# Low weight parts of the q, k and v projections by an accumulating transfer from GpSimd, high products first

## The chip, the cores and the metric

The kernel runs on one core of one Trainium2 chip. The metric is the device time of one execution in microseconds; several executions are timed and their median is given. A profile of one more execution shows what each engine did: PE (TensorE, matmuls), PEld (its weight loads), DVE (VectorE), ACT (ScalarE), POOL (GpSimd) and SP (SyncE, which here only issues DMAs).

## The reference

One encoder block with two token mixers side by side (a gated delta rule in both directions and a Fourier mixer), merged by gates, and an MLP with squared ReLU. T = 256 tokens, width 2048, all in float32. What bears on this case is the projection of the normed input and the delta rule branch:

```python
h = rms_norm(x, g_mix[l])
proj = h @ w_in[l]
q, k, v, z, f, scal, gates = jnp.split(proj, SPLIT_POINTS, axis=-1)
y_a = gated_deltanet_branch(q, k, v, z, scal, conv_w[l], ...)
...
# in the branch: convolution over 5 tokens, silu, heads of 128, then per chunk
m = jnp.where(strict, jnp.einsum("bhnid,bhnjd->bhnij", kb, k) * decay, 0.0)
a_mat = m + jnp.eye(CHUNK, dtype=m.dtype)
rhs = jnp.concatenate([v * beta, kb * jnp.exp(gc)[..., None]], axis=-1)
sol = lax.linalg.triangular_solve(a_mat, rhs, left_side=True, lower=True, unit_diagonal=True)
```

q, k and v have 1024 columns each, in 8 heads of 128.

## The kernel before

**Split products.** Each float32 matrix is split into a high part in fp32r (a rounded copy) and a low part (the rest), and a product is made of three: high by high, high by low and low by high. The input's parts are `h_hi` and `h_lo`. The weights come in pieces of 512 KB (128 x 1024 elements): SP loads a piece into a tile `raw`, `split` (L87) makes `hi` on ScalarE by a copy (L88) and `lo` on VectorE as raw - hi (L92), and PE multiplies. `wtiles` (L96) gives the tiles: four buffers for `raw`, three for `hi`, three for `lo`, shared by all the projections in turn.

**The q, k and v projections** are made by `pair_fm` (L104) for two head tiles at a time. A head tile has 2048 x 128 weights, two pieces (q = 0 and 1), and each piece 24 products of 128 x 256 that accumulate into one half of a PSUM bank: for each of 8 blocks L121 (high by high), L122 (high by low) and L127 (low by high). Five chunks of four heads come this way (40 pieces, 960 matmuls); the first chunk of k goes through `stream_k0` and isn't touched. `qkv_chunk` (L307) takes the sums from PSUM (L321), with GpSimd's memsets of the borders of `u` ahead of that, and convolves on ScalarE and VectorE (L324, L326). `stream` (L156) makes the other projections: z, the gates, and more.

**The delta rule** works on two groups of four heads (`dn_group`, L618). For each, `dn_k`, `dn_v` and `dn_q` project and norm, `dn_decay` makes the decays E, and `dn_inv` (L443) inverts the blocks: products of k (L463), the compact matrix Kc goes out to DRAM and comes back as Mf (L474, L481), 31 steps of two VectorE instructions (L489, L491) solve the 32 x 32 blocks, the solution Xf goes out and back as Xh (L493, L498), becomes Xc (L500), De and DT (L505 to L508), and PE joins the blocks (L521, L528, L540, L544), with copies between (L524, L532). `dn_out` (L560) makes the outputs (L574 to L601). z is projected between the groups (`z_chunk`).

**What sets the order.** The framework's scheduler orders each engine's instructions by a plan of its own before the program is built, across all of these functions. On the chip each engine works through its list in order, and waits at the first instruction whose inputs or buffers aren't ready. So a change in one function moves instructions of others too.

Of the kernel before, what the change touches and what calls it, by code (L numbers as in the profile page):

```python
# [8 lines left out]
F32 = mybir.dt.float32  # L9
F32R = mybir.dt.float32r  # L10
AF = mybir.ActivationFunctionType
ALU = mybir.AluOpType
PSUM = bass.MemoryType.PSUM

P = 128
# [12 lines left out]
def encoder_block_kernel(ctx, tc, xT, x, g_mix, w_qkv, w_k0, w_in, w_g, w_sc, conv_w, hprm, g_head, w_dn, w_fo, w_o,  # L28
                         g_mlp, w_up, w_down, g_fin, tri, dft, out, dbg=None):
    nc = tc.nc  # L30
    dve, act, pool, pe = nc.vector, nc.scalar, nc.gpsimd, nc.tensor
# [13 lines left out]
    def mm_ps():  # L45
        return psm.tile([P, NW], F32, tag="mm", name=nm("mm"))
# [40 lines left out]
    def split(hi, lo, src, scale=1.0, src2=None):  # L87
        act.activation(hi, src, AF.Copy, scale=scale)  # L88
        if src2 is None:
            src2 = src  # L90
        if isinstance(scale, float) and scale == 1.0:
            dve.tensor_tensor(lo, src2, hi.bitcast(F32), op=ALU.subtract)  # L92
        else:
            dve.scalar_tensor_tensor(lo, src2, scale, hi.bitcast(F32), op0=ALU.mult, op1=ALU.subtract)

    def wtiles(a=KP, n=NW, parts=True):  # L96
        raw = st.tile([P, a, n], F32, tag="raw", bufs=4, name=nm("raw"))
        if not parts:
            return raw, None, None
        hi = st.tile([P, a, n], F32R, tag="hi", bufs=3, name=nm("hi"))  # L100
        lo = st.tile([P, a, n], F32R, tag="lo", bufs=3, name=nm("lo"))
        return raw, hi, lo

    def pair_fm(srcs, ahi, alo):  # L104

        nk = srcs[0].shape[1]
        ps = mm_ps()
        last = None
        for j, src in enumerate(srcs):
            o = ps[:, j * T:j * T + T]  # L110
            for q in range(nk // 8):
                raw, hi, lo = wtiles()
                nc.sync.dma_start(raw.rearrange("p a b -> p (a b)"),
                                  src.rearrange("p k n -> p (k n)")[:, q * 1024:q * 1024 + 1024])
                split(hi, lo, raw)
                hv = hi.rearrange("p a b -> p (a b)")
                lv = lo.rearrange("p a b -> p (a b)")
                for kk in range(8):
                    k = 8 * q + kk
                    cs = slice(kk * P, kk * P + P)  # L120
                    first = pe.matmul(o, hv[:, cs], ahi[:, k, :], start=(k == 0), stop=False)  # L121
                    pe.matmul(o, hv[:, cs], alo[:, k, :], start=False, stop=False)  # L122
                    if last is not None:
                        tc.add_manual_dep(first.ins, last.ins.name, mybir.DependencyInfo(
                            mybir.DependencyClass.NoSync, mybir.DependencyReason.DATA), reason="one group at a time")
                        last = None
                    end = pe.matmul(o, lv[:, cs], ahi[:, k, :], start=False, stop=(k == nk - 1))  # L127
            last = end
        return ps

# [176 lines left out]
    def qkv_chunk(c, ps=None):  # L307

        u = pd.tile([P, 4, T + 4], F32, tag="u", bufs=1, name=nm("u"))
        pool.memset(u[:, :, 0:2], 0.0)  # L310
        pool.memset(u[:, :, T + 2:T + 4], 0.0)
        y = pd.tile([P, 4, T], F32, tag="y", bufs=1, name=nm("y"))
        done = 0
        while done < 4:
            if ps is None:
                p = pair_fm([w_qkv[4 * c + done], w_qkv[4 * c + done + 1]], h_hi, h_lo)
                p = p.rearrange("p (a b) -> p a b", a=2)
            else:
                p = ps[done]
            n = p.shape[1]  # L320
            dve.tensor_tensor(u[:, done:done + n, 2:T + 2], p, rbc.unsqueeze(1).to_broadcast([P, n, T]), op=ALU.mult)  # L321
            for j in range(done, done + n):
                cb = 4 * c + j
                act.activation(y[:, j, :], u[:, j, 0:T], AF.Copy, scale=cw[:, cb, 0:1])  # L324
                for w in range(1, 5):
                    dve.scalar_tensor_tensor(y[:, j, :], u[:, j, w:w + T], cw[:, cb, w:w + 1], y[:, j, :],  # L326
                                             op0=ALU.mult, op1=ALU.add)
            done += n
        return y
# [376 lines left out]
    for c in range(2):  # L706
        ps = stream(w_in[2 + c], KD, h_hi, h_lo)
        cs = slice(c * NW, c * NW + NW)
# [9 lines left out]
    for gr in range(8):  # L718
        pa = aux_ps()
        gs = slice(gr * P, gr * P + P)  # L720
        last = None
        for e in range(2):
            o = pa[:, e * T:e * T + T]
# [5 lines left out]
            last = pe.matmul(o, f_lo[:, e, gs], d_hi[:, e, :], start=False, stop=True)  # L729
# [5 lines left out]
        for s in range(2):  # L735
            cs = slice(s * P, s * P + P)
            for (lw, rw) in ((d_hi, ab_hi), (d_lo, ab_hi), (d_hi, ab_lo)):
                pe.matmul(pr, lw[:, 2, cs], rw.rearrange("p (e s m) -> p s e m", e=2, s=2)[:, s],  # L738
                          start=(n == 0), stop=(n == 5))
# [230 lines left out]
```

## Time and profile before

| | us |
|---|---|
| median of 3 runs | 1395.71 (1392.36 to 1395.87) |
| the profiled execution | 1394.12 |
| its span | 1392.4 |
| stretch of the q, k and v pieces on PE | 32.7 to 190 |
| stretch of z, the first gates and the rest of dn | 190 to 330 |

A page of the profile first gives the busy time of each engine, then the chain of work that ended last, followed back from the last instruction (its shares by engine tell what bounds the kernel), and then groups of instructions: line, engine, operation, output<-inputs, shapes and count, then the busy time, the mean in ns, and the idle time in front of them with what ended it. Other views of the trace give single rows (start and duration in us, with idle time ahead and its releaser in brackets), what each engine waited for, and tables by stretch.

### The profile page before, as it was taken

Reading aid. Unit: us, or ns where it says so; the run is one execution under the profiler, and the core shown is the slowest. Engines: PE = TensorE matmul, PEld = TensorE weight load, DVE = VectorE, ACT = ScalarE, POOL = GpSimd, SP = SyncE. Lnnn points to the kernel's source line nnn. Section 1 sums busy time; section 2 is a strip of 40 time slices with the busy share of each in tenths; the row PEclk is TensorE's granted clock in tenths of the full one; section 3 lists DMA queues with packets and bytes.
Section 4 is the critical chain, followed back from the end, with each engine's and each line's share of the span. In section 5 each row is a group of like instructions: output and inputs, shape, how many; then the busy total and the mean of one; then the engine's idle time right before and its main releaser. Section 6 shows DMA issues by size and latency. Waiting matters only on the chain.

```text
span 1392.4 us, 20162 instructions
## 1 busy us (share of the span) xinstructions
PE 1378.0 (99%) x7838; PEld 1198.8 (86%) x7838; DVE 864.9 (62%) x1239; ACT 689.1 (49%) x1042; POOL 35.9 (3%) x60
## 2 busy tenths in 40 slices
PE   9999999999999999999999999999999999999997
PEld 9999997888888888888888888888888888888897
DVE  7869997755556555655666665444456666644553
ACT  6586746454444444455554554333344555444442
POOL 2001110100000000000000000000000000000000
PEclk9999999999999999999999999999999999999999
DMA  8456466354566556676555556666655555666663
GB/s 289 150 167 180 154 165 175 92 166 138 176 200 181 157 176 191 193 266 191 174 195 191 192 192 185 195 196 192 191 192 191 194 189 183 194 191 192 195 198 119
DMA packets 94544, 255.63 MB, mean 184 GB/s; under 512 B 25456, under 2 KB 33648, under 8 KB 94064
## 3 DMA queue, kind: packets, MB, share of 16 engines
q1 hardware_dynamic: 93456, 250.15, 58.8%
q10 hardware_dynamic: 992, 4.19, 0.8%
q8 instruction: 61, 1.00, 0.3%
q14 instruction: 35, 0.29, 0.1%
HBM read 251.16 MB, written 3.15 MB: 183 GB/s over the span
## 4 chain that ended last, share of the span: by engine, by line
PE 94%; DMA 1%; issue 1%; DVE 1%; SPq 1%; ACT 1%; POOLq 0%; POOL 0%; DVEq 0%; ACTq 0%
PE mm L146 17%; PE mm L169 10%; PE mm L168 10%; PE mm L170 10%; PE mm L149 9%; PE mm L831 8%; PE mm L829 8%; PE mm L830 8%; PE mm L122 3%; PE mm L121 3%; PE mm L127 3%; DVE lo L92 0%; DMA raw<-in_w_k_dram 0%; PE aux L738 0%; SPq L481 0%
## 5 line engine op out<-in xcount | busy, mean ns | idle before, releaser
L92 DVE TENSOR_TENSOR lo<-raw,hi 128x1024 fp32r<-128x1024 f32 (+1 forms) x459 | 560.5, 1222 | 337.5 <-ACT hi L88 329.2
L88 ACT ACTIVATE hi<-raw 128x1024 fp32r<-128x1024 f32 (+1 forms) x459 | 485.8, 1059 | 417.5 <-PE mm L831 185.8
L146 PE MATMUL mm<-hh,hi 128*128 128x512 f32 x1024 | 245.0, 391 | 0.0
L146 PEld LDWEIGHTS mm<-hh,hi 128*128 128x128 f32 x1024 | 188.0, 188 | 36.4
L830 PE MATMUL mm<-lo,rh 128*128 128x512 f32 (+1 forms) x512 | 192.3, 376 | 0.0
L831 PE MATMUL mm<-hi,rl 128*128 128x512 f32 (+1 forms) x512 | 192.3, 376 | 0.0
L829 PE MATMUL mm<-hi,rh 128*128 128x512 f32 (+1 forms) x512 | 173.7, 376 | 0.0
L169 PE MATMUL mm<-lo,hh 128*128 128x512 f32 x384 | 152.2, 396 | 0.0
L170 PE MATMUL mm<-hi,hh 128*128 128x512 f32 x384 | 151.6, 395 | 0.0
L168 PE MATMUL mm<-hi,hh 128*128 128x512 f32 x384 | 143.0, 393 | 0.6 <-ACT merged L655 0.4
L149 PEld LDWEIGHTS mm<-hh,lo 128*128 128x128 f32 x1024 | 131.5, 191 | 5.1
L149 PE MATMUL mm<-hh,lo 128*128 128x256 f32 x1024 | 133.1, 283 | 0.0
L830 PEld LDWEIGHTS mm<-lo,rh 128*128 128x128 f32 x512 | 96.4, 188 | 17.6
L831 PEld LDWEIGHTS mm<-hi,rl 128*128 128x128 f32 x512 | 96.3, 188 | 17.4
L829 PEld LDWEIGHTS mm<-hi,rh 128*128 128x128 f32 x512 | 96.2, 188 | 17.4
L153 ACT COPY rt<-mm 128x256 f32<-128x256 f32 x64 | 23.8, 372 | 164.5 <-PE mm L146 164.5
L154 DVE TENSOR_TENSOR rt<-mm,rt 128x256 f32<-128x256 f32 x64 | 27.2, 425 | 110.5 <-ACT rt L153 110.5
L122 PE MATMUL mm<-hh,hi 128*128 128x256 f32 x320 | 90.5, 283 | 0.0
L121 PE MATMUL mm<-hh,hi 128*128 128x256 f32 x320 | 90.4, 283 | 0.0
L127 PE MATMUL mm<-hh,lo 128*128 128x256 f32 x320 | 90.3, 283 | 0.0
L168 PEld LDWEIGHTS mm<-hi,hh 128*128 128x128 f32 x384 | 72.4, 189 | 15.9 <-ACT hi L88 0.6
L169 PEld LDWEIGHTS mm<-lo,hh 128*128 128x128 f32 x384 | 72.7, 189 | 14.5
(310 smaller groups left out, 1673.8 us busy)
## 6 DMA issues: line engine op xcount, KB each, us to landing
raw<-in_w_up_dram SPq DMA_DIRECT2D x128, 512.0 KB, 4.0
raw<-in_w_down_dram SPq DMA_DIRECT2D x128, 512.0 KB, 3.5
raw<-in_w_g_dram SPq DMA_DIRECT2D x64, 512.0 KB, 3.9
raw<-in_w_qkv_dram SPq DMA_DIRECT2D x40, 512.0 KB, 4.4
raw<-in_w_in_dram SPq DMA_DIRECT2D x32, 512.0 KB, 4.1
raw<-in_w_o_dram SPq DMA_DIRECT2D x32, 512.0 KB, 3.8
raw<-in_w_dn_dram SPq DMA_DIRECT2D x16, 512.0 KB, 3.5
raw<-in_w_fo_dram SPq DMA_DIRECT2D x16, 512.0 KB, 3.6
```

The source lines that it names most:

```text
L88: act.activation(hi, src, AF.Copy, scale=scale)
L92: dve.tensor_tensor(lo, src2, hi.bitcast(F32), op=ALU.subtract)
L121: first = pe.matmul(o, hv[:, cs], ahi[:, k, :], start=(k == 0), stop=False)
L122: pe.matmul(o, hv[:, cs], alo[:, k, :], start=False, stop=False)
L146: pe.matmul(ps, hv[:, cs], ab[:, k].rearrange("p a b -> p (a b)"), start=(k == 0), stop=(k == KD - 1))
L149: pe.matmul(ps[:, 0:T], lv[:, cs], ab[:, k, 0], start=False, stop=False)
L168: pe.matmul(ps[tb], ah, hi[:, kk, :], start=(k == 0), stop=False)
L169: pe.matmul(ps[tb], ah, lo[:, kk, :], start=False, stop=False)
L170: pe.matmul(ps[tb], al, hi[:, kk, :], start=False, stop=(k == nk - 1))
L829: pe.matmul(ps[tb], ah, hi[:, kk, :], start=(k == 0), stop=False)
L830: pe.matmul(ps[tb], ah, lo[:, kk, :], start=False, stop=False)
L831: pe.matmul(ps[tb], al_, hi[:, kk, :], start=False, stop=(k == 31))
```

## The change

The pieces with q = 1 (20 of 40) no longer get their low part from VectorE. ScalarE makes the high part as before, and a second copy with scale -1 into `lo`; then a DMA issued by GpSimd adds `raw` to `lo` in place. For all 40 pieces the 16 products with high weight parts now stand first, and the 8 with low parts behind them. Lines behind the change are 9 higher afterwards (L321 becomes L330, L491 becomes L500, L521 becomes L530).

```diff
-                split(hi, lo, raw)
                 hv = hi.rearrange("p a b -> p (a b)")
                 lv = lo.rearrange("p a b -> p (a b)")
-                for kk in range(8):
-                    k = 8 * q + kk
-                    cs = slice(kk * P, kk * P + P)
-                    first = pe.matmul(o, hv[:, cs], ahi[:, k, :], start=(k == 0), stop=False)
-                    pe.matmul(o, hv[:, cs], alo[:, k, :], start=False, stop=False)
...
-                    end = pe.matmul(o, lv[:, cs], ahi[:, k, :], start=False, stop=(k == nk - 1))
+                if q == 0:
+                    split(hi, lo, raw)
+                else:
+                    act.activation(hi, raw, AF.Copy)
+                    act.activation(lo, raw, AF.Copy, scale=-1.0)
+                    pool.dma_start(lo.bitcast(F32), raw, accum_op=ALU.add)
+                for part in range(2):
+                    for kk in range(8):
+                        k = 8 * q + kk
+                        cs = slice(kk * P, kk * P + P)
+                        if part == 0:
+                            first = pe.matmul(o, hv[:, cs], ahi[:, k, :], start=(k == 0), stop=False)
+                            pe.matmul(o, hv[:, cs], alo[:, k, :], start=False, stop=False)
...
+                        else:
+                            end = pe.matmul(o, lv[:, cs], ahi[:, k, :], start=False, stop=(k == nk - 1))
```

In the rows below, a name such as `lo_980` is one use of a buffer; the number only tells the uses apart, and differs between the two kernels.

On PE, at the end of the first q = 1 piece (high part hi_979, low part lo_980) and the start of the next, before:

```order
L121 MATMUL mm_947<-hh,hi_979 128x256
L122 MATMUL mm_947<-hh,hi_979 128x256
L127 MATMUL mm_947<-hh,lo_980 128x256
L121 MATMUL mm_947<-hh,hi_1009 128x256
L122 MATMUL mm_947<-hh,hi_1009 128x256
```

and at the end of such a piece now (hi_1040 and lo_1041, then hi_1083):

```order
L128 MATMUL mm_947<-hh,hi_1040 128x256
L129 MATMUL mm_947<-hh,hi_1040 128x256
L136 MATMUL mm_947<-hh,lo_1041 128x256 x8
L128 MATMUL mm_1081<-hh,hi_1083 128x256
L129 MATMUL mm_1081<-hh,hi_1083 128x256
```

Low products stood after every second high one; now eight stand together at a piece's end.

On VectorE, some steps of the solve of group 0, before:

```order
L489 TENSOR_TENSOR tf_719<-Mf_717,Xf_718 128x136
L92 TENSOR_TENSOR lo_2702<-raw_2700,hi_2701 128x1024
L491 TENSOR_TENSOR Xf_718<-Xf_718,tf_719 128x17x8
L489 TENSOR_TENSOR tf_719<-Mf_717,Xf_718 128x128
L491 TENSOR_TENSOR Xf_718<-Xf_718,tf_719 128x16x8
L489 TENSOR_TENSOR tf_719<-Mf_717,Xf_718 128x135
L92 TENSOR_TENSOR lo_2764<-raw_2762,hi_2763 128x1024
L491 TENSOR_TENSOR Xf_718<-Xf_718,tf_719 128x15x9
L92 TENSOR_TENSOR lo_2794<-raw_2792,hi_2793 128x1024
```

and the same steps now:

```order
L498 TENSOR_TENSOR tf_719<-Mf_717,Xf_718 128x136
L500 TENSOR_TENSOR Xf_718<-Xf_718,tf_719 128x17x8
L498 TENSOR_TENSOR tf_719<-Mf_717,Xf_718 128x128
L500 TENSOR_TENSOR Xf_718<-Xf_718,tf_719 128x16x8
L498 TENSOR_TENSOR tf_719<-Mf_717,Xf_718 128x135
L500 TENSOR_TENSOR Xf_718<-Xf_718,tf_719 128x15x9
L498 TENSOR_TENSOR tf_719<-Mf_717,Xf_718 128x126
```

The three subtractions between and behind these steps are gone; over the whole solve of group 0 there were 22, and there are 6.

The first product with De of group 0 stood, on PE, among the pieces of the first gates (mm_3357), before:

```order
L170 MATMUL mm_3057<-hi_3185,hh 128x512
L521 MATMUL dn_822<-De,grp_528 32x32 x16
L169 MATMUL mm_3357<-lo_3361,hh 128x512
```

and stands now inside the last piece of q (lo_3005), ahead of the second z chunk (mm_3076, mm_3077):

```order
L136 MATMUL mm_2911<-hh,lo_3005 128x256 x3
L530 MATMUL dn_822<-De,grp_528 32x32
L136 MATMUL mm_2911<-hh,lo_3005 128x256 x5
L177 MATMUL mm_3076<-hi_3079,hh 128x512
L178 MATMUL mm_3076<-lo_3080,hh 128x512
```

It has moved ahead by about a z chunk. On GpSimd, the last three DMAs before that place stand like this, in a queue that held no DMA before:

```order
L122 DMA lo_2871<-raw_2869 128x1024
L122 DMA lo_2944<-raw_2942 128x1024
L392 TENSOR_TENSOR nk_2191<-sk_2171,pex 128x8
L319 MEMSET u_2773 128x4x2
L320 MEMSET u_2773 128x4x2
L122 DMA lo_3005<-raw_3003 128x1024
```

The last transfer is queued behind nk (the norms of k in group 1) and the memsets of u.

More of the change, by code (lines that the diff above doesn't have):

```diff
@@ L114, in pair_fm @@
                                   src.rearrange("p k n -> p (k n)")[:, q * 1024:q * 1024 + 1024])
-                split(hi, lo, raw)
                 hv = hi.rearrange("p a b -> p (a b)")
                 lv = lo.rearrange("p a b -> p (a b)")
-                for kk in range(8):
-                    k = 8 * q + kk
-                    cs = slice(kk * P, kk * P + P)
[L121 to L126, printed above, removed]
-                    end = pe.matmul(o, lv[:, cs], ahi[:, k, :], start=False, stop=(k == nk - 1))
+                if q == 0:
[11 more added lines that the diff above has]
+                            pe.matmul(o, hv[:, cs], alo[:, k, :], start=False, stop=False)
+                            if last is not None:
+                                tc.add_manual_dep(first.ins, last.ins.name, mybir.DependencyInfo(
+                                    mybir.DependencyClass.NoSync, mybir.DependencyReason.DATA),
+                                    reason="one group at a time")
+                                last = None
+                        else:
+                            end = pe.matmul(o, lv[:, cs], ahi[:, k, :], start=False, stop=(k == nk - 1))
             last = end
```

## The prediction

> **What bounds the kernel now.** I read the head of the page first, then its chain of work that ended last, then the table of stretches, and only then single rows. The profiled execution took 1394.12 us; its span is 1392.4, so 1.7 us lie around it.
>
> ```profile
> span 1392.4 us, 20162 instructions
> PE 1378.0 (99%) x7838; PEld 1198.8 (86%) x7838; DVE 864.9 (62%) x1239; ACT 689.1 (49%) x1042; POOL 35.9 (3%) x60
> PE 94%; DMA 1%; issue 1%; DVE 1%; SPq 1%; ACT 1%; POOLq 0%; POOL 0%; DVEq 0%; ACTq 0%
> L122 PE MATMUL mm<-hh,hi 128*128 128x256 f32 x320 | 90.5, 283 | 0.0
> L92 DVE TENSOR_TENSOR lo<-raw,hi 128x1024 fp32r<-128x1024 f32 (+1 forms) x459 | 560.5, 1222 | 337.5 <-ACT hi L88 329.2
> L88 ACT ACTIVATE hi<-raw 128x1024 fp32r<-128x1024 f32 (+1 forms) x459 | 485.8, 1059 | 417.5 <-PE mm L831 185.8
> ```
>
> TensorE is the bound: 99% busy, 94% of the chain. The table of stretches (length, then busy time and count on PE, PEld, DVE, ACT and POOL, granted clock, DMA share, GB/s) tells where anything is to be had. The q, k and v pieces run from 32.7 to 190 us.
>
> ```profile
> 32.70:70.00 37.30, 37.30 (x278) 35.63 (x278) 32.55 (x75) 20.08 (x44) 3.66 (x4) 1.00 0.51 153
> 70.00:110.00 40.00, 40.00 (x277) 37.25 (x277) 28.76 (x47) 31.00 (x65) 5.66 (x5) 1.00 0.50 161
> 110.00:150.00 40.00, 40.00 (x334) 39.87 (x333) 37.24 (x75) 27.27 (x63) 2.57 (x7) 1.00 0.66 178
> 150.00:190.00 40.00, 40.00 (x332) 39.71 (x331) 39.08 (x76) 25.62 (x57) 7.15 (x6) 1.00 0.51 160
> 190.00:230.00 40.00, 38.84 (x294) 31.40 (x293) 32.13 (x65) 25.96 (x57) 1.64 (x1) 0.96 0.65 172
> 230.00:270.00 40.00, 36.90 (x247) 31.62 (x246) 33.39 (x97) 17.19 (x39) 3.71 (x9) 0.96 0.39 117
> ```
>
> VectorE is nearly full in 110 to 190 (37.24 and 39.08 of 40), yet PE is busy the whole of these four stretches at clock 1.00. A freed VectorE cannot shorten them. Only the 80 us behind them lose time: PE is short by 1.16 + 3.10 = 4.26 us, and a clock of 0.96 over 80 us is another 3.2. **The gain is thus at most about 7.5 us**, and it lies wholly behind the changed code. The waits of PE there show its cause, the block inverse of the delta rule (dn):
>
> ```profile
> PE dn L540 <- DVE DT L532: 1.0, 1, 1.0
> PE dn L528 <- ACT W L524: 0.8, 1, 0.8
> 214.17 0.39 PE L169 MATMUL mm<-lo,hh 128*128 128x512 f32 x1
> 214.39 0.39 PE L170 MATMUL mm<-hi,hh 128*128 128x512 f32 x1
> 222.14 0.63 PE L169 MATMUL mm<-lo,hh 128*128 128x512 f32 x1
> 222.57 0.63 PE L170 MATMUL mm<-hi,hh 128*128 128x512 f32 x1
> ```
>
> The lower four rows are two pairs of equal products: 0.22 us from start to start ahead of the L528 wait, 0.43 behind it. That is where the clock of 0.96 comes from: half speed for a few matmuls after the small dn products and their waits.
>
> **The change part by part.** Products: 24 per piece as before, 128x256 each, in another order. They accumulate in the same PSUM bank, so PE's work is unchanged:
>
> ```profile
> 179.82 0.28 PE L121 MATMUL mm<-hh,hi 128*128 128x256 f32 x1
> 179.94 0.28 PE L122 MATMUL mm<-hh,hi 128*128 128x256 f32 x1
> ```
>
> 0.12 us from start to start, 2.9 us per piece, before and after.
>
> VectorE: 20 subtractions of L92 go, 20 x 1.222 = 24.4 us. ScalarE: 20 copies with scale -1 come, priced as L88, 20 x 1.059 = 21.2 us. It is busy 20.08 + 31.00 + 27.27 + 25.62 = 104 of 157 us there, and 125 afterwards; thinnest in 70 to 110, where four or five new copies make 31 into 36 of 40. PE's work hides it, so I cost it at 0; without that cover 2 us.
>
> The transfer is the unknown: 512 KB from SBUF to SBUF, read twice (raw and lo) and written once, issued by GpSimd. No row shows such a one. The nearest are the loads of the same tile:
>
> ```profile
> raw<-in_w_qkv_dram SPq DMA_DIRECT2D x40, 512.0 KB, 4.4
> DMA to landing us min/median/max: 3.5/4.4/6.0
> 199.14 0.17 DVE L491 TENSOR_TENSOR Xf<-Xf,tf 128x16 f32<-128x16 f32 x1
> 199.67 0.38 SPq L493 DMA_DIRECT2D dscr<-Xf  x1
> ```
>
> From below: 4.4 us, as if the second read were free. From above: 8.8, two such passes one after the other. I take the middle, 6.6, since the second read is neither free nor a pass with its own write. What it costs follows from the room it has. The slot of a low tile comes free with the last low product of the piece three earlier (three buffers). With nothing else between, PE then still has 48 + 16 products, 64 x 0.12 = 7.7 us, until it wants the new low part. Of these the copy takes 1.06 and the hand-over to the queue 0.36 (199.31, the end of L491, to 199.67), which leaves **6.3 us for the transfer**. In the new order most pieces have other products between: counted row by row with that spacing (and 0.22 for 128x512) the 20 rooms run from 7.7 to 12.4 us, nine of them under 8.6. At 4.4 nothing stalls; at 6.6 only the two tightest, 0.3 us each, so 0.6, and I write 0.8; at 7.8 about 6 us; at 8.8 the shortfalls add up to 21, of which about 12 remain, because a stall at one piece gives the next transfer as much more time.
>
> A page of the Trainium skill, DMA: Bandwidth & Descriptors, section Anatomy of one DMA, puts a transfer from GpSimd at 2.0 us plus its bytes by 436 GB/s. By that rule the 512 KB would be an estimated 3.2 us, below even the loads' median of 4.4 here; the sum would then have no stall at all, and 1389 instead of 1390.
>
> GpSimd itself issues 20 transfers. It is busy 3.66 + 5.66 + 2.57 + 7.15 = 19 of 157 us, so it has the time, but its queue is in order. At the last piece of q, nk and two memsets of u stand ahead of the transfer, and wait for the convolution on VectorE. The convolution's rows stand behind the last step of the solve, so it is done about 6 us after that step, by the times below at about 182 us, and PE wants the low part at 189: 7 us, enough for 6.6, and no more. The raw tile is held until the transfer lands; SP's loads behind it wait by so much longer; with four raw buffers they have, by the same count of products, about 6 us to spare, and that covers transfers up to about 8 us.
>
> What is gained, the tail. The matrix solve of group 0 (31 steps of L489 and L491) and what follows it:
>
> ```profile
> 129.14 0.21 DVE L489 TENSOR_TENSOR tf<-Mf,Xf 128x31 f32<-128x31 f32 x1 [2.25 <-DMA Mf<-dscr]
> 214.71 0.66 PE L521 MATMUL dn<-De,grp 32*32 32x32 f32 x30
> ```
>
> The solve took 70 us (129.14 to 199.31) because 22 subtractions stood between its steps, and 15.4 us passed from its end to L521 (store, loads back, Xc, transposes). The new order leaves 6 subtractions between the steps, and puts L521 (now L530) into the last piece of q, about 25 us earlier, at 189.5. When will De be there? Freed of 16 subtractions (20 us), the solve ends between 179 (70 less 20 from 129.14) and 176 (when its last subtraction, of lo_2914, has its slot: piece 2810's low products leave PE at about 171, and the rows behind it take 5 us). Plus 15.4 gives 191.5 to 194.5. I take the earlier, since with so few rows the slot and not VectorE is last: PE waits 2 us. In exchange the dn_out products no longer stand almost back to back but among the gates' pieces, where their waits are covered. The tail's loss falls from 7.5 to 2 us: **-5.5 us**. Sum: -5.5 + 0.8 = -4.7, that is 1394.1 - 4.7 = 1389.4 against the profiled time; the median shown, 1395.71, is 1.6 above that execution, and from it the sum gives 1391.0. I say **1390**.
>
> **The rivals.** (a) The transfer takes the place of the subtraction as what PE waits for, at every second piece. It decides from 7.8 us on, where stalls (6) eat the gain (5.5). At 8.8 they are 12, net +6.5, so 1401, and with waits on the raw tiles behind it 1405. For it: two reads, an instruction that no row shows, and GpSimd and VectorE disturbing each other:
>
> ```profile
> 152.66 0.77 DVE L489 TENSOR_TENSOR tf<-Mf,Xf 128x120 f32<-128x120 f32 x1
> 152.19 1.10 POOL L437 TENSOR_SCALAR_AFFINE_SELECT E<-E 128x1024 f32<-128x1024 f32 x1 [4.18 <-ACT E L434]
> 182.00 2.92 DVE L449 TENSOR_TENSOR E<-E,cn 128x1024 f32<-128x1024 f32 x1
> 180.92 2.92 POOL L451 TENSOR_TENSOR E<-E,cn 128x1024 f32<-128x1024 f32 x1 [3.61 <-DVE cn L395]
> ```
>
> A 128x1024 operation of VectorE, 1.22 us in the group of L92, took 2.92 beside one of GpSimd. If issuing is held back in the same way, by an operation or two of VectorE of 1.22 us, 6.6 becomes 7.8 to 9.0. Against it: VectorE has fewer of these now, and the rooms are wider than the tightest. The Trainium skill, SBUF — State Buffer, in section SBUF: two separate sides, in its box on the "DVE blocks DMA" trap, says that GpSimd writes the descriptors of its transfers itself and is locked out while VectorE holds the port they share; the trace agrees as far as operations go (2.92 against 1.22), and for transfers no run here shows it yet. (b) The tail is not cured: De comes at 194.5 or later, PE waits 5 us at L530 instead of 2, and the 2.5 to 4 us of half clock and of the later waits (3.2 for the clock before) stay: 1394 to 1396, no change. It decides when the solve ends after 179. For it: PE's order moved by 25 us, the solve by 20 to 23. Against it: behind L530 there is a whole z chunk over which the later waits are spread. (c) The DMA engines fill up. In 150 to 190 a share of 0.51 moves 160 GB/s, so a pass of 512 KB takes all engines 1.7 us, and a transfer 1.7 to 3.3. Twenty are 0.21 to 0.43 of the 157 us, on a mean share of 0.55: not full. Only if each took 4.4 us of all engines would the mean be 1.1 and the stage 16 us longer: 1410 upwards. (d) ScalarE becomes the bound in 70 to 110: +2 to +4, 1392 to 1394. That nothing of the change comes about is out: the order shows its instructions.
>
> **How the numbers follow.** Forecast 0.38, late transfers (a) 0.27, uncured tail (b) 0.24, full DMA engines (c) 0.07, ScalarE (d) 0.04. The forecast alone reaches from 1386 (all of 7.5 gained) to 1393. The range takes in (b) and (a) up to its bound: 1384 to 1410, the lower end a little beyond 7.5 because modelled ends of matmuls can hide idle time. 0.3% is 4.2 us, about what a measurement of this kernel can tell from no change. Faster by more: the forecast and a little of (b), 0.40. Slower: (a), (c), the end of (b), 0.36. Within: 0.24.
>
> **What would show it.** The landing time of lo<-raw from GpSimd against 6.3; waits of PE at L136 on it (forecast: two or three, under 1 us in sum; (a): at ten or more places); VectorE down by about 24 us and ScalarE up by 21 in 32 to 190; the solve's last step near 176 and PE's first L530 near 190 with a wait of 2 us; clock and PE busy time in 190 to 270 near 1.00 and 39 of 40. A transfer over 7.8 us makes the prediction wrong, as does a wait of 5 us or more at L530.

## The result, and the profile after

The changed kernel takes 1409.78 us (median; 1406.94 to 1412.09) against 1395.43 before: a ratio of 1.0104, 95% interval 1.0092 to 1.0116. It is slower by 1%, where the forecast said faster by 0.3 to 0.4%. The profiled execution took 1408.62, its span is 1406.8.

From the page of the changed kernel, the head, the chain and the rows of the new operations (for DMAs: size and the median from issue to landing in us):

```profile
span 1406.8 us, 20215 instructions
PE 1380.4 (98%) x7838; PEld 1200.8 (85%) x7838; DVE 845.4 (60%) x1219; ACT 707.4 (50%) x1062; POOL 53.7 (4%) x80
q0 software_dynamic: 2880, 10.49, 4.0%
PE 88%; DMA 5%; issue 3%; DVE 2%; ACT 2%; SPq 1%; POOL 0%; POOLq 0%; DVEq 0%; ACTq 0%
raw<-in_w_qkv_dram SPq DMA_DIRECT2D x40, 512.0 KB, 4.9
lo<-raw POOLq DMA_DIRECT2D x20, 512.0 KB, 6.6
```

PE's share of the chain fell from 94% to 88%, and DMA's rose from 1% to 5%. VectorE is 19.5 us less busy and ScalarE 18.3 us more (24.4 and 21.2 were forecast). The table by stretch of the changed kernel (columns as in the prediction):

```profile
32.70:70.00 37.30, 35.71 (x271) 34.15 (x271) 29.52 (x77) 22.74 (x46) 6.14 (x7) 1.00 0.74 198
70.00:110.00 40.00, 36.10 (x235) 32.70 (x234) 19.60 (x36) 31.76 (x64) 4.76 (x7) 1.00 0.66 184
110.00:150.00 40.00, 37.99 (x291) 37.79 (x292) 21.43 (x30) 23.75 (x52) 7.44 (x8) 0.91 0.89 189
150.00:190.00 40.00, 34.16 (x260) 32.95 (x259) 33.16 (x88) 30.57 (x59) 10.32 (x13) 0.96 0.82 222
190.00:230.00 40.00, 37.51 (x374) 33.46 (x373) 35.22 (x71) 27.16 (x60) 5.69 (x6) 1.00 0.90 212
230.00:270.00 40.00, 40.00 (x249) 34.08 (x248) 35.73 (x84) 18.69 (x35) 1.67 (x1) 1.00 0.49 143
```

The tail did what was forecast: in 190 to 270 PE lacks 2.5 us and the clock is 1.00, where 7.5 us had been lost. But the four stretches before, in which PE had never waited, now lack 1.6 + 3.9 + 2.0 + 5.8 us, and two of them have a clock under 1. VectorE, which was to be relieved, is idle for half of 70 to 150, so it was not what the kernel lacked. PE's waits, the transfers on GpSimd (duration of the issuing instruction in ns: least, median, most), their landing, and ScalarE's waits for loads between 30 and 230 us:

```profile
PE mm L136 <- DMA lo<-raw: 10.7, 6, 3.9
PE aux L378 <- ACT offk L566: 3.3, 1, 3.3
PE aux L378 <- ACT off L475: 1.1, 1, 1.1
PE dn L530 <- DVE De L514: 0.8, 1, 0.8
...
L122 POOL DMA_DIRECT2D lo<-raw x20: 850/864/1062, 31.5 to 202.2; - x20
DMA to landing us min/median/max: 4.5/6.6/10.3
...
ACT hi L120 <- DMA raw<-in_w_qkv_dram: 8.4, 2, 6.4
ACT hi L88 <- DMA raw<-in_w_qkv_dram: 4.8, 3, 2.2
ACT hi L88 <- DMA raw<-in_w_in_dram: 4.3, 2, 2.7
```

The median landing is the 6.6 us that the forecast took. Single ones took up to 10.3, and six of the 20 pieces make PE wait, 10.7 us in all. ScalarE, which before has no row for such a wait in this stretch, now stands 17.5 us for loads: the loads are late as well.

### The profile page after: what moved, and what is told of

Read it like the earlier page. It is cut to its first block, busy times and chain, and to the rows that moved or that the text cites. A ratio compares the mean times of both kernels' runs of the same rounds, so it can differ in the third digit from the quotient of the medians.

```text
span 1406.8 us, 20215 instructions
## 1 busy us (share of the span) xinstructions
PE 1380.4 (98%) x7838; PEld 1200.8 (85%) x7838; DVE 845.4 (60%) x1219; ACT 707.4 (50%) x1062; POOL 53.7 (4%) x80
## 4 chain that ended last, share of the span: by engine, by line
PE 88%; DMA 5%; issue 3%; DVE 2%; ACT 2%; SPq 1%; POOL 0%; POOLq 0%; DVEq 0%; ACTq 0%
PE mm L155 17%; PE mm L179 10%; PE mm L177 10%; PE mm L178 10%; PE mm L158 9%; PE mm L840 8%; PE mm L838 8%; PE mm L839 8%; DMA lo<-raw 3%; DMA raw<-in_w_qkv_dram 1%; PE mm L136 1%; PE mm L128 1%; PE mm L129 1%; DVE lo L92 1%; DMA raw<-in_w_k_dram 0%
## 5 line engine op out<-in xcount | busy, mean ns | idle before, releaser
L92 DVE TENSOR_TENSOR lo<-raw,hi 128x1024 fp32r<-128x1024 f32 (+1 forms) x439 | 537.1, 1224 | 333.8 <-ACT hi L88 324.6
L88 ACT ACTIVATE hi<-raw 128x1024 fp32r<-128x1024 f32 (+1 forms) x439 | 464.6, 1059 | 395.7 <-PE mm L840 185.8
L158 PE MATMUL mm<-hh,lo 128*128 128x256 f32 x1024 | 133.2, 283 | 0.0
L839 PEld LDWEIGHTS mm<-lo,rh 128*128 128x128 f32 x512 | 96.4, 188 | 17.5
L177 PEld LDWEIGHTS mm<-hi,hh 128*128 128x128 f32 x384 | 72.2, 188 | 14.3
L179 PEld LDWEIGHTS mm<-hi,hh 128*128 128x128 f32 x384 | 72.3, 188 | 14.0
L128 PE MATMUL mm<-hh,hi 128*128 128x256 f32 x320 | 81.1, 289 | 0.0
L129 PE MATMUL mm<-hh,hi 128*128 128x256 f32 x320 | 80.9, 288 | 0.0
```

The source lines that it names most:

```text
L158: pe.matmul(ps[:, 0:T], lv[:, cs], ab[:, k, 0], start=False, stop=False)
L177: pe.matmul(ps[tb], ah, hi[:, kk, :], start=(k == 0), stop=False)
L179: pe.matmul(ps[tb], al, hi[:, kk, :], start=False, stop=(k == nk - 1))
L839: pe.matmul(ps[tb], ah, lo[:, kk, :], start=False, stop=False)
```

## The experiments

Every run is set against runs of the kernel before on the same chip. In the tables, "stage" is PE's idle time in 32.7 to 210 us plus the length times (1 - clock); "110 to 160" is the same for that part of it, and "tail" for 210 to 330. "Trip" runs from the start of the last copy that makes Kc (group 0) to the first step of the solve on VectorE, that is Kc's way to DRAM and back as Mf. All four columns come from the table by stretch and from rows of the traces, that is from the one profiled execution of each kernel. It took within about 2 us of the median, except in hold_twice (1396.94, 6 us under it) and half_piece (1407.82, 5 us over it).

| kernel | median us | ratio (95% interval) | stage | 110 to 160 | trip | tail |
|---|---|---|---|---|---|---|
| before | 1395.43 | | 0.0 | 0.0 | 10.9 | 7.9 |
| changed | 1409.78 | 1.0104 (1.0092 to 1.0116) | 19.5 | 10.3 | 21.1 | 1.6 |
| order_alone | 1389.55 | 0.9966 (0.9953 to 0.9979) | 0.1 | 0.1 | 11.3 | 3.5 |
| hold_alone | 1391.89 | 0.9978 (0.9969 to 0.9988) | 0.3 | 0.3 | 13.0 | 3.3 |
| hold_twice | 1402.98 | 1.0054 (1.0037 to 1.0070) | 1.4 | 0.9 | 15.4 | 8.4 |
| copy_alone | 1400.25 | 1.0042 (1.0028 to 1.0057) | 0.0 | 0.0 | 11.1 | 12.4 |
| every_fourth | 1396.26 | 1.0005 (0.9996 to 1.0014) | 4.7 | 4.2 | 14.1 | 2.5 |
| half_piece | 1403.02 | 1.0058 (1.0042 to 1.0075) | 11.3 | 11.0 | 21.3 | 9.7 |
| from_dram | 1407.09 | 1.0091 (1.0067 to 1.0114) | 19.1 | 4.1 | 14.8 | 0.5 |
| no_reader | 1411.89 | 1.0126 (1.0110 to 1.0141) | 20.5 | 10.7 | 20.2 | 2.9 |
| no_reader_dram | 1404.96 | 1.0075 (1.0058 to 1.0092) | 19.9 | 11.3 | 18.3 | 1.2 |
| transfer_alone | 1414.87 | 1.0133 (1.0118 to 1.0148) | 24.8 | 9.2 | 16.3 | 3.6 |
| late_low | 1411.51 | 1.0110 (1.0090 to 1.0130) | 22.6 | 7.5 | 18.3 | 2.1 |
| late_low_dram | 1399.26 | 1.0040 (1.0026 to 1.0053) | 12.5 | 4.8 | 17.6 | 0.0 |
| late_low_dve | 1399.99 | 1.0041 (1.0026 to 1.0056) | 0.1 | 0.1 | 10.8 | 16.5 |
| only_k | 1398.77 | 1.0037 (1.0023 to 1.0051) | 8.5 | 8.5 | 20.9 | 3.7 |

The "before" of each ratio was measured beside the run, 1393.7 to 1395.4 us. The scheduler plans each kernel anew, so the tail differs by several us between kernels that differ little; the column "stage" hardly does, with 0.0 to 1.4 us in all kernels of the table that have no accumulating transfer.

**order_alone.** The order of products without the transfers:

```diff
-                if q == 0:
+                if True:
                     split(hi, lo, raw)
```

> All 40 pieces get their low part from VectorE as before; only the products stand high first. Theory R (a transfer holds its raw tile until it lands, so SP's in-order loads and everything behind them come late) and theory L (the transfer lands later than the room that PE leaves, whatever the loads do) both expect the time of before within 0.3%, 1391 to 1400 us, and no wait of PE in the q, k, v pieces. Theory O (the order of the products itself costs) expects over 1400 us and waits of PE at L136.

It is faster than before by 0.34%, a little more than R and L expected, and PE loses only 0.1 us in the stage. The table by stretch of order_alone, behind the stage:

```profile
190.00:230.00 40.00, 39.22 (x313) 32.11 (x312) 34.04 (x67) 26.64 (x59) 0.68 (x1) 1.00 0.69 178
230.00:270.00 40.00, 37.24 (x257) 32.29 (x256) 35.22 (x105) 17.75 (x40) 4.50 (x11) 1.00 0.38 113
```

The clock is 1.00 where it was 0.96 twice, and PE lacks 3.5 us, not 4.3. So most of the gain in the tail that the forecast gave to the freed VectorE (5.5 us) came with the plan around the new order of products alone (the tail's loss goes from 7.9 to 3.5 us), and theory O falls. This is the fastest of all kernels run. The transfers, put on top of it, cost the changed kernel 20 us.

**hold_alone and copy_alone.** The transfer without a reader and with VectorE's subtraction kept, and the second copy without the transfer:

```diff
+                split(hi, lo, raw)
+                if q == 1:
+                    side = tc.dram_tile([P, KP, NW], F32, name=nm("side"))
+                    pool.dma_start(side, raw)
```

```diff
+                if q == 1:
+                    act.activation(lo, raw, AF.Copy, scale=-1.0)
+                split(hi, lo, raw)
```

> As order_alone, with a plain 512 KB transfer from each q = 1 raw tile to DRAM issued by GpSimd, which no product waits for; no second copy on ScalarE. R expects 1400 to 1407 us, with SP waiting 30 us or more on these transfers. L expects the time of order_alone within 3 us.

> As order_alone, with the second copy of ScalarE (lo = -hi) into each q = 1 low tile, which VectorE's subtraction then overwrites; no transfers. R and L expect the time of order_alone within 3 us. Theory C (ScalarE's 20 more copies are what makes it late) expects 1403 us or more.

hold_alone is 2.3 us slower than order_alone, its stage loses 0.3. These transfers land sooner, as the rows of hold_alone show (queue of GpSimd, then the landing):

```profile
q0 software_dynamic: 2880, 10.49, 2.0%
side<-raw POOLq DMA_DIRECT2D x20, 512.0 KB, 4.6
```

A plain transfer holds raw for 4.6 us, not 6.6, so this spoke against R without settling it. copy_alone missed what R and L expected: it is 10.7 us slower than order_alone, but in its stage PE loses nothing; nearly all of it (8.9 us) is in the tail, where the plan came out worse. For the stage of the changed kernel theory C falls.

**from_dram.** The transfer reads the weights again and raw is free early:

```diff
-                    pool.dma_start(lo.bitcast(F32), raw, accum_op=ALU.add)
+                    pool.dma_start(lo, src.rearrange("p k n -> p (k n)")[:, q * 1024:q * 1024 + 1024]
+                                   .rearrange("p (a b) -> p a b", a=KP), accum_op=ALU.add)
```

> The changed kernel, but the accumulating transfer reads the weights a second time from DRAM and not from raw, so raw is free after ScalarE's copies, and PE still waits for the transfer. R expects most of the loss to go: 1390 to 1399 us, and no SP wait on these transfers. L expects 1404 to 1413 us, with waits of PE at L136 as in the changed kernel (10.7 us).

The time came out as L said, and not as R did. The waits of PE and the landing in from_dram:

```profile
PE mm L137 <- DMA lo<-in_w_qkv_dram: 9.9, 10, 2.1
PE dn L531 <- DVE De L515: 3.8, 1, 3.8
...
DMA to landing us min/median/max: 6.2/8.3/10.6
```

It isn't clean: the transfer itself became longer (8.3 us for 6.6), so one limit was taken away and another made tighter.

**late_low, transfer_alone, hold_twice, every_fourth.** late_low gives the transfers to the first piece of a tile and puts its low products last; transfer_alone has the loop of before; hold_twice repeats hold_alone's transfer; every_fourth leaves 10:

```diff
-                for part in range(2):
+                for part, qq in (((0, 0),), ((0, 1), (1, 1), (1, 0)))[q]:
...
-                if q == 0:
+                if q == 0 or j == 0:
                     split(hi, lo, raw)
```

> As many transfers as in the changed kernel (20), but for the first piece of each head tile, and its eight low products stand at the tile's end, behind the second piece's. A transfer then has 96 products, 11.5 us, from the release of its slot to its first low product, not 64 (7.7). Theory L (PE waits because a transfer takes longer than its room) expects the waits of PE on lo<-raw to go from 10.7 us to under 2, and 1387 to 1394 us. Theory R (what counts is the raw tile held until the transfer lands, and the loads behind it) expects the hold and so most of the loss to stay: 1400 us or more.

> The transfers of the changed kernel, with the products in the order of before (each low product behind its two high ones), so that PE wants a low part two products into the piece and not sixteen: 50 products of room, 6.0 us. L expects another 14 x 0.12 = 1.7 us of wait at many of the 20 pieces, half of it made up at the next one: 1415 to 1430 us. R expects the time of the changed kernel within 4 us.

> As hold_alone, with two plain transfers of each q = 1 raw tile to DRAM one after the other, so that the tile is held about as long as in the changed kernel (6.6 us) and the DMA engines carry at least as much; PE waits for none of them. L expects the time of order_alone within 4 us (1386 to 1394). R, and a theory D that the DMA engines are simply too full, expect 1400 us or more.

> Only the second head tile of each pair gets its q = 1 low part by the transfer: 10 transfers, the rest as in order_alone. L expects some five waits of PE of 0 to 2 us with their half clock behind: half of the loss, 1393 to 1401 us. R expects more than half of the loss to go, as SP's loads then have a piece more to recover: 1389 to 1393 us.

late_low is where L fell: with half as much room again the loss stayed (22.6 us in the stage). PE waited less for transfers and more for others, in late_low's row of waits:

```profile
PE mm L136 <- DMA lo<-raw: 6.7, 4, 2.8
PE aux L379 <- ACT offk L567: 4.4, 1, 4.4
PE dn L531 <- DVE De L515: 3.0, 1, 3.0
```

transfer_alone, just under the lower end of what L expected (1415), shows that less room does cost: 14.6 us of waits for transfers at ten places. hold_twice fell between: its median is slower as R and D had it, but in the profiled execution the stage lost only 1.4 us, with the DMA engines at a share of 0.99 in 110 to 150 and SP waiting 78 us for held raw tiles. So in that execution neither full engines nor held tiles made PE late, while VectorE made the low parts; where the other three executions lost some 6 us more, no trace shows. every_fourth lost 4.7 us in the stage, nearly all beside the trip. Its time is in L's range and beyond R's, but with one wait for a transfer (1.8 us) and not five.

**no_reader, late_low_dram, late_low_dve, half_piece.** no_reader takes away PE's wait; late_low_dram joins the edits of late_low and from_dram, late_low_dve is the control without transfers; half_piece moves half of each low part:

```diff
-                            end = pe.matmul(o, lv[:, cs], ahi[:, k, :], start=False, stop=(k == nk - 1))
+                            end = pe.matmul(o, (lv if q == 0 else hv)[:, cs], ahi[:, k, :], start=False, stop=(k == nk - 1))
```

```diff
+                    act.activation(lo[:, 1], raw[:, 1], AF.Copy, scale=-1.0)
+                    pool.dma_start(lo[:, 1].bitcast(F32), raw[:, 1], accum_op=ALU.add)
+                    dve.tensor_tensor(lo[:, 0], raw[:, 0], hi[:, 0].bitcast(F32), op=ALU.subtract)
```

> The changed kernel with its 20 transfers, copies and held raw tiles, but the low products of the q = 1 pieces read the high part instead, so that no product waits for a transfer; as many products (the low correction of those pieces is left out). Theory L (PE's own wait for the low part is the loss) expects 1386 to 1394 us. Theory R (raw is held, loads come late, ScalarE stands behind them) expects 1402 to 1410 us, with waits of PE on hi or on the copies of dn.

> late_low, with the transfers reading DRAM and not raw: both the longer room (11.5 us) and raw free after ScalarE's copies. Theory B (two rings of buffers are each too short for a transfer, the four raw and the three low tiles, so that relaxing one alone gains nothing) expects 1388 to 1396 us and under 2 us of waits on transfers. Theory D (the DMA engines are too full, loads and transfers hold each other up) expects 1402 us or more.

> The order of products of late_low with all low parts by VectorE, no transfers: a control. All theories of the transfers expect 1387 to 1395 us. If it is over 1400, late_low's order itself costs and late_low tells nothing of its room.

> The changed kernel with half of each q = 1 low part (the last four of eight blocks) by a transfer of 256 KB and the first half by VectorE: 20 transfers of half the size, 12 us off VectorE. D and B expect landings near 5 us and 1391 to 1400 us, about half of the loss; a theory that the number of transfers counts and not their bytes (GpSimd's issue, fixed costs) expects 1403 us or more.

no_reader decides against the rival of the prediction as it was put. No product waits for a transfer, and the time is that of the changed kernel (1411.89). Its waits of PE:

```profile
PE aux L378 <- ACT offk L566: 6.2, 1, 6.2
PE aux L378 <- ACT aux L362: 4.7, 2, 4.0
PE dn L530 <- DVE De L514: 2.2, 1, 2.2
PE mm L178 <- DVE lo L92: 1.7, 2, 1.3
```

Ahead of 110 us it loses nothing, where the changed kernel lost 5.5; behind it the lateness is back, as a wait for ScalarE's and VectorE's work on dn. half_piece kept more than half of the loss (11.3 of 19.5 in the stage, in the profiled execution); its median is 3 us beyond what D and B expected and just at the 1403 of the theory of counts, and decides nothing. late_low_dram had the least time of the kernels with 20 accumulating transfers, but 1399 is beyond what B expected and short of D's 1402, and the control missed too (a tail of 16.5 us): its order of products came with a bad plan, so of late_low only the stage says something.

**Five raw tiles.** There is room for a fifth raw tile only if one of the three high tiles is given up, in the whole kernel:

```diff
-        raw = st.tile([P, a, n], F32, tag="raw", bufs=4, name=nm("raw"))
+        raw = st.tile([P, a, n], F32, tag="raw", bufs=5, name=nm("raw"))
...
-        hi = st.tile([P, a, n], F32R, tag="hi", bufs=3, name=nm("hi"))
+        hi = st.tile([P, a, n], F32R, tag="hi", bufs=2, name=nm("hi"))
```

> The changed kernel with five raw tiles, for which one of the three high tiles is given up (there is no room for both), everywhere in the kernel. Theory R (the four raw tiles are the ring that is too short while transfers hold them) expects PE's idle time in 33 to 210 us to fall from 14 us to under 6, ScalarE's waits on loads from 17 us to under 6, and a time at least 7 us under after_hi2's. Theory D (full DMA engines) expects idle time over 10 us and the time of after_hi2 within 3 us.

> The changed kernel with two high tiles instead of three: what giving one up costs. R and D expect 1409 to 1425 us, and idle time of PE in 33 to 210 us of 14 us or more.

> order_alone with two high tiles, no transfers: the control for both. Expected 1390 to 1402 us; raw5_hi2 within 5 us of it would mean that R accounts for nearly all of the loss.

They came to 1431.8, 1430.64 and 1416.65 us (ratios 1.0261, 1.0260 and 1.0147), the two controls beyond what was expected of them. The high tile costs 27 us by itself (order_hi2 against order_alone), and against after_hi2 the fifth raw tile gained nothing. ScalarE's waits for loads went (no such row is left, after 6.3 and 2.6 us in after_hi2), but PE then waited 14.5 us for transfers. Its idle time in 33 to 210 us was 19.7 us, after 18.5 in after_hi2 (whose profiled execution was 10 us over its median), so this came out as D expected and not as R did. late_low_raw5, late_low with the same two edits, was as slow (1429.84), slower than B had it, and its 15.7 us of idle time are again D's. All three pay for the high tile, so they weigh little.

> late_low (11.5 us of room) with five raw tiles and two high ones, transfers from raw: both rings longer, and only the high tile given up against it. B expects PE's idle time in 33 to 210 us under 8 us (15.5 in late_low, 19.7 in raw5_hi2), but no good time, because of the high tile: 1405 to 1425 us. D expects 13 us or more of idle time.

**no_reader_dram.** Neither a reader nor a held raw tile, the rest kept (the edits of no_reader and from_dram):

> no_reader, with the transfers reading DRAM and not raw: no product waits for a transfer, and no raw tile is held by one; the same copies, the same number of transfers and more traffic on the DMA engines (the low correction of the q = 1 pieces is left out). Theory B (both rings count: the held raw tiles and PE's wait for the low tile, each of which loses the time alone) expects PE's idle time in 33 to 210 us under 4 us (13.4 in no_reader, 13.8 in from_dram) and 1387 to 1397 us. Theory D (full DMA engines) expects over 10 us and 1402 us or more; theory C (ScalarE's copies) expects the same as D, with waits of PE on ScalarE.

B falls by this: the stage lost 19.9 us, 12.8 of them idle time. That and the time are what D and C expected. C alone is excluded for the stage by copy_alone; D isn't excluded. The waits of PE in no_reader_dram, VectorE's first, and the store of Kc:

```profile
PE aux L379 <- ACT offk L567: 7.3, 1, 7.3
PE dn L531 <- DVE De L515: 5.0, 1, 5.0
...
DVE tf L499 <- DMA raw<-in_w_qkv_dram: 9.2, 1, 9.2
...
L484 SPq DMA_DIRECT2D dscr<-Kc x1: 330/330/330, 123.7 to 123.7; - x1
DMA to landing us min/median/max: 5.4/5.4/5.4
```

The DVE row is the first step of the solve. It names a weight load, but the step starts at 141.46, when the last of Mf's loads has landed (141.4). VectorE stood 9.2 us there, in order, with dn's products behind it. That pointed to the trip, and its column shows it: 10.8 to 11.3 us without transfers on GpSimd, 13.0 and 15.4 with plain ones, 14 to 21 with accumulating ones. No raw tile is held by a transfer here, and the store of Kc is issued as soon as Kc is there (123.7); yet it takes 5.4 us to land, where it takes 2.0 in order_alone.

**only_k.** Transfers only in the four pieces beside the trip:

```diff
-                if q == 0:
+                if q == 0 or not moved:
                     split(hi, lo, raw)
...
-                p = pair_fm([w_qkv[4 * c + done], w_qkv[4 * c + done + 1]], h_hi, h_lo)
+                p = pair_fm([w_qkv[4 * c + done], w_qkv[4 * c + done + 1]], h_hi, h_lo, c == 3)
```

> Transfers only in the four q = 1 pieces of the second k chunk, beside which the compact matrix Kc of group 0 goes out and comes back as Mf; the other 36 pieces as in order_alone. Theory M (loads that wait for transfers stand in SP's queue ahead of the Kc store, the Mf loads and the next weights; VectorE and ScalarE then wait in order, and PE for their copies) expects Kc to the first step of the solve to take 15 us or more (21.1 in the changed kernel, 11.3 in order_alone), 4 us or more of PE idle in 110 to 160 us, and 1394 to 1402 us. Theory N (all 20 transfers add up, each costing its share of the 20 us between order_alone and the changed kernel) expects a fifth: 1391 to 1395 us, a round trip under 14 us, and under 3 us of PE idle there.

The time, the trip and the idle time came out as theory M had them: four transfers of 20 cost 9.2 us against order_alone (1398.77 and 1389.55), and the stage's loss, 8.5 us, is all in 110 to 160. The waits of PE in only_k, SP's rows in this place, and the first step of the solve:

```profile
PE mm L136 <- DMA lo<-raw: 3.5, 1, 3.5
PE aux L378 <- ACT offk L566: 1.5, 1, 1.5
...
114.39 9.68 SPq L113 DMA_DIRECT2D raw<-in_w_qkv_dram  x3
124.16 0.38 SPq L483 DMA_DIRECT2D dscr<-Kc  x1
124.63 0.38 SPq L113 DMA_DIRECT2D raw<-in_w_qkv_dram  x1
129.44 8.51 SPq L490 DMA_DIRECT2D Mf<-dscr  x8
...
141.51 0.21 DVE L498 TENSOR_TENSOR tf<-Mf,Xf 128x31 f32<-128x31 f32 x1 [11.06 <-DMA raw<-in_w_qkv_dram]
```

The waits are not those of theory M alone. Of PE's 5.0 us of idle time, 3.5 are its own wait for a transfer that took 9.8 us to land, and 1.5 the wait for ScalarE's copy of dn that M named; the other 3.4 us of the loss are half clock. So only_k doesn't price the path through the trip by itself.

Kc was ready at about 121. Its store is issued at 124.16, behind loads that wait for raw tiles held by transfers, and lands 5.2 us later (2.0 in order_alone). The trip can be taken apart in this way in every trace (us; the 0.4 us of the last copy into Kc make up the sum):

| kernel | Kc ready to issue of its store | issue to landing | landing to the first step of the solve |
|---|---|---|---|
| order_alone | 0.0 | 2.0 | 8.8 |
| hold_twice | 0.2 | 4.6 | 10.2 |
| no_reader_dram | 0.1 | 5.4 | 12.4 |
| only_k | 3.2 | 5.2 | 12.1 |
| changed | 3.7 | 5.8 | 11.1 |

Only the first column is time in SP's queue behind a held raw tile: 3.2 of the 9.6 us by which the trip of only_k is longer than that of order_alone, and 3.7 of 9.8 in the changed kernel. The rest is that the trip's own transfers are issued and land more slowly, and no_reader_dram has that without any held tile. The DMA engines had a share of 0.58 in 110 to 160 in order_alone and of 0.74 to 0.97 in the other four. That their being full is the reason is likely, but not shown: hold_twice has the highest share and the shortest of the four longer trips.

## Why the prediction was wrong, point by point

The step that failed is the +0.8 us for stalls in the forecast's sum, and with it the raw tiles and the start of the solve (129.14), which it took as undisturbed, at no cost. The runs show 19.5 us in its place: 14.2 us of idle PE, of which 10.7 are waits for transfers and 3.3 a wait for a copy behind the late trip, and the half clock behind the stalls. With the tail's loss at 1.6 us (6.3 less) the same sum gives 1394.1 - 6.3 + 19.5 = 1407.3, against 1408.62 profiled.

**The same place in the changed kernel** shows how one late transfer reaches PE twice. SP's queue, then PE, VectorE and ScalarE, from the trace of the changed kernel:

```profile
128.29 5.67 SPq L113 DMA_DIRECT2D raw<-in_w_qkv_dram  x2
134.05 1.09 SPq L483 DMA_DIRECT2D dscr<-Kc  x1
139.92 5.72 SPq L490 DMA_DIRECT2D Mf<-dscr  x8
145.74 3.43 SPq L113 DMA_DIRECT2D raw<-in_w_qkv_dram  x4
...
133.65 1.22 PE L136 MATMUL mm<-hh,lo 128*128 128x256 f32 x8 [2.01 <-DMA lo<-raw]
151.00 0.21 DVE L498 TENSOR_TENSOR tf<-Mf,Xf 128x31 f32<-128x31 f32 x1 [5.90 <-DMA raw<-in_w_qkv_dram]
152.11 1.06 ACT L120 ACTIVATE hi<-raw 128x1024 fp32r<-128x1024 f32 x1 [6.38 <-DMA raw<-in_w_qkv_dram]
154.96 0.70 ACT L566 COPY offk<-aux 128x256 f32<-128x256 f32 x2
155.37 0.40 PE L378 MATMUL aux<-q,k 128*128 128x256 f32 x1 [3.27 <-ACT offk L566]
```

A transfer issued at 123.33 lands at 133.6, after 10.3 us. PE waits for it (2.01). It also holds its raw tile, so SP's second load stands until 133.6, and the Kc store, ready at 130, behind it until 134.05. The store itself takes 5.8 us to land, not 2.0. Mf comes back late, the weights behind Mf's eight loads as well; ScalarE stands 6.38 us for them in its order with the copy offk behind it, and PE waits 3.27 us for that copy.

- **The transfer's price** was right in the median: 6.6 us from issue to landing, as taken. As the middle between two bounds, 4.4 and 8.8, it was so partly by luck. Its work on the DMA engines, 4.0% of the span by 20, is 2.8 us of all 16, inside the 1.7 to 3.3. By the rule of the Trainium skill in DMA: Bandwidth & Descriptors, section Anatomy of one DMA (an estimated 3.2 us), there would have been no stall; the rows speak against it, with 4.5 us as the least of 20 landings.
- **The room at PE** failed as a step. "At 6.6 only the two tightest, 0.3 us each" put one number against rooms counted from a release on time. Landings spread from 4.5 to 10.3. At the six places where PE waited it was ready 5.2 to 8.3 us behind the issue, and the transfer took 6.7 to 10.3; three of them, with landings of 8.7, 9.4 and 10.3, make 7.5 of the 10.7 us that PE waited, not 0.8.
- **The held raw tile** is the step that was wrong in kind: "with four raw buffers they have, by the same count of products, about 6 us to spare, and that covers transfers up to about 8 us". The count was of weights alone. In the same queue stand the Kc store and the loads of Mf, and behind them VectorE and ScalarE wait in order. But the queue is only 3.7 of the 9.8 us by which the trip grew; that the trip's own transfers land more slowly beside the accumulating ones is the larger part, and the forecast has no term for it.
- **Half clock.** The forecast priced it for the tail and not for new stalls. The changed kernel's clock cost about 5 us in the stage: three stretches of 3.4 us at half speed.
- **ScalarE and the freed VectorE.** Costed at 0 and hidden: copy_alone's stage loses nothing. The solve did shrink as forecast, from 70 to 44.6 us (151.0 to 195.6), and 15 us passed from its end to L530, as forecast. But it began 22 us late, so nothing of that reached PE in the stage.
- **The tail** came as forecast in size (2.5 us lost, forecast 2) but not for its reason: order_alone has a tail of 3.5 us with all subtractions on VectorE. L530 came at 210.54, 21 us later than forecast, with a wait of 0.82, not 2.
- **The rivals.** (a) had the sign and, with 1401 to 1405, nearly the size, but partly by luck: its condition, transfers of 7.8 us, did not hold for the median, waits came at six places and not ten, and without any such wait the time stays (no_reader). Of VectorE holding up GpSimd's issue, the trap named by the Trainium skill in SBUF — State Buffer, section SBUF: two separate sides, there is no sign: the issue took 0.85 to 1.06 us at all 20 places. (c) was dismissed as "not full" at a mean share of 0.55 + 0.21 to 0.43; it was 0.66 to 0.90 by stretch, full for short times. hold_twice, at 0.99, lost 1.4 us in the stage of its profiled execution, which speaks against full engines as the cause by themselves; that they make landings slower stays open. (b): its condition came, as the solve ended after 179, but PE was late too and waited 0.82 us. (d) did not occur.

**What is shown and what isn't.** Shown: the accumulating transfers, not the order of products (order_alone) nor the second copies alone (copy_alone), cost the time in the stage. PE's own wait for them can be taken away and the time stays (no_reader), and with no raw tile held either the stage's loss stays (no_reader_dram): then PE waits for ScalarE's and VectorE's work behind the late trip. In the changed kernel the loss in 110 to 160 (10.3 us) is about half from waits for transfers and half from that path (3.3 us and the half clock behind it). The 5.5 us ahead of 110 and nearly all of the 3.4 behind 160 are waits for transfers. Not settled: why single landings took 9 to 10 us and others under 5, how much of the slower landings is full DMA engines, and what would remain with a fifth raw tile and three high ones, for which there is no room.

## What to carry to other kernels

An engine that is 98% busy in a stretch in which the bound engine never waits isn't worth relieving there: look first whether the bound engine loses anything, and try the reordering that comes with an idea without the idea itself (here 0.34% faster alone, 1% slower with it). A transfer that takes the place of a compute instruction holds its source for longer, so count the ring of that buffer too, and everything that shares the queue which refills it, small round trips above all. Set the spread of its landings, not their median, against the room, and ask what lands later beside it. When a wait is removed and the time stays, look for the queue in which the lateness travels.

## What the runs showed of the hardware

An accumulating transfer of 512 KB within SBUF took the DMA engines twice the time of a plain one (4.0% against 2.0% of the span for 20, the latter from SBUF to DRAM in hold_alone; also 4.0% with DRAM as the source, in from_dram), and 6.6 against 4.6 us to land.

Half speed of PE followed stalls in the changed kernel of 3.90, 2.01 and 3.27 us, each time for about 3.4 us, and did not follow those of 1.59 and 1.63 us. That is no fixed bound: in every_fourth it followed one of 1.75 us, in from_dram none of 1.75 and 1.87, and in only_k none of 2.47. In the table of five-us stretches of the changed kernel, the stall before 109.87 and what follows it:

```profile
105.00:110.00 5.00, 1.10 (x9) 0.79 (x8) 2.56 (x7) 4.29 (x9) 0.86 (x1) 1.00 0.80 219
110.00:115.00 5.00, 5.00 (x30) 5.00 (x31) 4.12 (x3) 2.84 (x7) 3.83 (x2) 0.66 0.95 206
115.00:120.00 5.00, 5.00 (x44) 5.00 (x44) 1.56 (x3) 2.50 (x3) 0.88 (x1) 1.00 0.86 256
```

0.34 of 5 us is 1.7 us lost, 3.4 us at half speed, on top of the stall itself. Thirty matmuls fall in the second stretch and 44 in the third.
